# Second LoRA products and the mLSTM broadcast in float32r parts in a hybrid RWKV-7 / mLSTM trunk

## The chip, the core and the metric

The kernel runs on one core of one Trainium2 chip. TensorE multiplies matrices, VectorE (DVE in the profile), ScalarE (ACT) and GpSimd (POOL) work element by element, and DMA queues, most of them fed by SyncE (SP), move data between DRAM and the on-chip memory. The metric is the device time of one execution in microseconds; times below are those of one core.

## What is computed

One layer of a streaming encoder for 2,048 prompt frames behind 16 meta tokens and for 8 streams of 16 new frames: a norm and a combined projection, RWKV-7 time mixing (8 heads of 64) beside an mLSTM (4 heads of 128), an output projection, and a gated feed-forward part. The parts that the change touches, cut from the reference:

```python
def rwkv7_mix(p, shift_prev, S0, mu, w0, w2, a0, a2, g2, ...):
    pm = p + (prev - p) * mu                      # prev: p one token earlier
    r, k, v = pm[..., :i1], pm[..., i1:i2], pm[..., i2:i3]
    wl, al, gl = pm[..., i3:i4], pm[..., i4:i5], pm[..., i5:]   # 64, 64, 128 columns
    w = -softplus(-(w0 + tanh(wl) @ w2)) - 0.5
    decay = exp(-exp(w))
    a = sigmoid(a0 + al @ a2)
    g = sigmoid(gl) @ g2
    ...
    S = S * w_t + sa * (kk_t * a_t) + v_t * k_t   # one token after the other

def mlstm_block(state, blk):
    ...
    inter = b + m[..., None]
    mt = maximum(inter, max(Dm, axis=-1))         # running maximum
    wi = exp(Dm - mt[..., None])
    s = einsum('bhtd,bhjd->bhtj', q, k) * wi
    ...
```

The products with `w2`, `a2` and `g2` are "the second LoRA products". `mt` enters the mLSTM's weights as one row that stands for all rows of a block, which the kernel brings about by a product on TensorE ("the broadcast").

## The kernel before

The kernel has two phases. The first computes both mixers and ends at about 1,865 us of the profile, the second the feed-forward part; the change touches the first alone. Its tokens are cut into six segments: segment 0 with the 8 streams and the first frames (272 columns, 320 with padding), segments 1 to 5 with 384. Each segment has four slots, and slot u handles one pair of RWKV heads. Pair and segment together are called a unit here, numbered 0 to 23 (unit 11 is pair 3 of segment 2).

Large products are made in float32r, a form of float32 whose products appear as one record each. An operand is split in two parts, `hi` (a cast to float32r) and `lo` (the rest), and hi x hi, hi x lo and lo x hi are added up in one bank (L320). Weights are split once, by a cast on ScalarE (L374) and a subtraction on VectorE, and the parts are kept in DRAM. A product of plain float32 operands, such as the second LoRA products (L627, L631, L635) and the broadcast (L955), appears as two records in the profile.

A unit runs through these steps:

- **Front** (`rwkv`): projections of k, r and v (L320), and the three second LoRA products: `pw` (L627) and `pa` (L631) with 64 rows each, `pg` (L635) with 128. Their weights `lw2` lie on the chip for the whole run. Their moving operands `lo1` and `lo2` are made at the segment's first slot.
- **Scores**: three groups of two chunks of 64 tokens. A group's scores come from TensorE through the one bank of ring `a` into a buffer `sc` of ring `scs` (six buffers); its diagonal 16 x 16 blocks are masked into `dg` (L718) and added up into `cm` (L720), both on VectorE.
- **Forward substitution**: the diagonal blocks go through DRAM to another layout (`ad`, L750, and `bt`, L751, both issued by SyncE), GpSimd inverts them in 15 steps of a product and a subtraction (L759, L761), and the result goes back through DRAM (`td`, L764, and `ct`, L766) into `TA` (GpSimd, L775 by the helper L259).
- **Levels** (`levels`): two steps that extend the inverses from 16 to 64 rows. TensorE multiplies `cL` and `TA` (L305), the product is copied into `wv` (two buffers, L252), and TensorE multiplies it with `TA` again. A unit of segments 1 to 5 has six `wv` tiles.
- **Chain** (`chain`): for each chunk in turn the products with the state, L826, L839 and L845. This part and the levels are written in the program at the start of the slot after the unit's own, ahead of the next unit's front.

The mLSTM part of a slot runs over blocks of 128 tokens (64 for part of segment 0). L954 makes the scores, L955 the broadcast: a column of the identity with 4 rows, repeated over the columns, times the 4 rows of `ng`. There are 76 broadcasts.

The order of the instructions on each engine is not written out: a scheduler decides it before the run from priorities, which the table `KN` moves by stage. On the chip each engine takes its instructions in that fixed order and waits where data or a buffer isn't ready. Tiles of one tag share a ring of buffers; a tile that takes a buffer waits until the last reader of the tile that had it before.

The lines on which the change acts most:

```python
T.matmul(pw[:, :m], lw2[0:64, 0, us], lo1[0:64, :m], start=True, stop=True)
T.matmul(pa[:, :m], lw2[64:128, 0, us], lo1[64:128, :m], start=True, stop=True)
T.matmul(pg[:, :m], lw2[:, 1, us], lo2[:, :m], start=True, stop=True)
dg = sp.tile([128, 2, 4, 16], F32, name="dg", tag="dg", bufs=1)
wv = sp.tile([128, 2, 64], F32, name="wv", tag="wv")
```

## Time and profile before

| | |
|---|---|
| time, median of 3 runs (lowest to highest) | 3524.24 us (3522.81 to 3527.25) |
| span of the profiled execution | 3507.6 us |
| TensorE busy | 3411.7 us, 97% of the span |
| VectorE, ScalarE, GpSimd busy | 2146.4, 1152.2 and 941.0 us |
| moved by DMA | 459.40 MB, 131 GB/s in the mean |
| chain that ended last | TensorE 86%, VectorE 6%, DMA 3% |

The span runs from the first to the last instruction of one profiled execution; the median is 16.6 us longer. A timeline gives the start and the duration of an instruction (or of several alike, with their count); since products overlap in TensorE's pipeline, what one costs is the distance from its start to the next start, not its duration. Windows give the busy time of the engines in a stretch and the granted clock, as a share of full speed.

### The profile page before, as it was taken

The page shows a single profiled execution, that of the slowest core. Times are in us where ns is not written, and L with a number is a line of the kernel's source. Part 1 is how long each engine was busy: PE and PEld are TensorE (multiplying, and loading weights), DVE is VectorE, ACT ScalarE, POOL GpSimd, SP SyncE. Part 2 cuts the span into 40 slices and gives each one's busy share as a digit, 9 for nine tenths or more (in the row PEclk, how much of TensorE's full clock was granted, in tenths as well). Part 3 has the DMA queues.
Part 4 walks back from the last instruction along what each step waited for, and adds up shares of the span by engine and source line. Part 5 has one row for each costly group of instructions (what it writes and reads, how often), then busy time and mean ns, then how long its engine had stood idle before and what let it go on. Part 6 is the DMA issues. An engine that isn't in the chain of part 4 may idle for free.

```text
span 3507.6 us, 63114 instructions
## 1 busy us (share of the span) xinstructions
PE 3411.7 (97%) x24228; PEld 3123.6 (89%) x24228; DVE 2146.4 (61%) x5529; ACT 1152.2 (33%) x2826; POOL 941.0 (27%) x2294
## 2 busy tenths in 40 slices
PE   7999999999999999999989999999999999999998
PEld 6776888888888888888878999999999999999998
DVE  7777767666665776766665555574545447454544
ACT  5443444333433343343332222232222223222222
POOL 2532335434334444434421000021000012010002
PEclk9888999999999999999988999999999999999999
DMA  8753666455455545545523222232222233212221
GB/s 307 252 172 109 218 221 202 150 171 179 148 164 172 174 151 186 184 142 195 167 85 110 76 79 73 73 113 84 67 66 67 66 127 111 66 48 67 67 67 63
DMA packets 187565, 459.40 MB, mean 131 GB/s; under 512 B 68320, under 2 KB 111744, under 8 KB 156800
## 3 DMA queue, kind: packets, MB, share of 16 engines
q1 hardware_dynamic: 136648, 187.25, 18.0%
q0 software_dynamic: 28080, 204.48, 17.6%
q10 hardware_dynamic: 22536, 63.63, 4.8%
q8 instruction: 191, 3.13, 0.4%
q14 instruction: 110, 0.90, 0.1%
HBM read 381.68 MB, written 73.63 MB: 130 GB/s over the span
## 4 chain that ended last, share of the span: by engine, by line
PE 86%; DVE 6%; DMA 3%; ACT 2%; issue 1%; POOL 1%; ACTq 0%; SPq 0%; POOLq 0%; DVEq 0%
PE ps_gm L320 43%; PE ps_iv L320 11%; PE ps_a L320 10%; PE ps_m L320 5%; PE ps_iv L305 2%; PE ps_a L712 2%; PE ps_ch L826 1%; PE ps_ch L845 1%; PE ps_ch L839 1%; PE ps_iv L810 1%; PE ps_m L955 1%; DVE w L259 1%; DMA xt<-in_x_dram 1%; PE ps_a L305 1%; PE ps_m L972 1%
## 5 line engine op out<-in xcount | busy, mean ns | idle before, releaser
L320 PE MATMUL ps_gm<-hhi,w 128*128 128x384 f32 (+1 forms) x2976 | 813.1, 345 | 7.4 <-ACT w L374 2.2
L320 PE MATMUL ps_gm<-h2hi,w 128*128 128x384 f32 (+1 forms) x2816 | 701.1, 327 | 0.2 <-ACT ub L1221 0.2
L320 PEld LDWEIGHTS ps_gm<-hhi,w 128*128 128x128 f32 x2976 | 540.8, 193 | 30.2 <-issue 5.5
L320 PE MATMUL ps_gm<-hlo,w 128*128 128x384 f32 (+1 forms) x1488 | 502.2, 338 | 3.0 <-DVE hlo L360 3.0
L320 PEld LDWEIGHTS ps_gm<-h2hi,w 128*128 128x128 f32 x2816 | 500.0, 188 | 0.9 <-ACT ub L1221 0.5
L320 PE MATMUL ps_gm<-h2lo,w 128*128 128x384 f32 (+1 forms) x1408 | 459.9, 327 | 0.0
L374 ACT CAST w<-wraw 128x1024 fp32r<-128x1024 f32 (+2 forms) x291 | 259.4, 892 | 455.8 <-PE ps_iv L320 243.0
L320 PE MATMUL ps_iv<-gh,w 128*128 128x384 f32 (+1 forms) x1410 | 361.2, 330 | 0.0
L320 PE MATMUL ps_a<-h2hi,w 128*128 128x384 f32 (+1 forms) x1408 | 358.0, 327 | 0.0
L259 DVE TENSOR_TENSOR w<-wraw,w 128x1024 fp32r<-128x1024 f32 (+2 forms) x291 | 301.0, 1035 | 64.4 <-ACT w L374 60.4
L320 PEld LDWEIGHTS ps_gm<-hlo,w 128*128 128x128 f32 x1488 | 287.3, 193 | 9.5 <-DVE hlo L360 3.4
L320 PEld LDWEIGHTS ps_gm<-h2lo,w 128*128 128x128 f32 x1408 | 264.9, 188 | 0.0
L320 PEld LDWEIGHTS ps_iv<-gh,w 128*128 128x128 f32 x1410 | 252.5, 188 | 0.0
L320 PEld LDWEIGHTS ps_a<-h2hi,w 128*128 128x128 f32 x1408 | 251.0, 188 | 0.1
L320 PE MATMUL ps_iv<-gw,w 128*128 128x384 f32 (+1 forms) x705 | 232.6, 330 | 0.0
L320 PE MATMUL ps_a<-h2lo,w 128*128 128x384 f32 (+1 forms) x704 | 230.5, 327 | 0.0
L1238 ACT ACTIVATE fth<-ac 128x384 f32<-128x384 f32 (+1 forms) x132 | 67.2, 510 | 398.1 <-DVE ac L1236 388.7
L1231 POOL COPY h_f<-ub 128x2 f32<-128x2 f32 x88 | 16.4, 187 | 636.7 <-DVE ub L252 403.9
L320 PE MATMUL ps_m<-gh,w 128*128 128x384 f32 (+1 forms) x702 | 186.0, 330 | 0.0
L1259 DVE TENSOR_TENSOR x<-x,ps_iv 128x384 f32<-128x384 f32 (+1 forms) x160 | 85.3, 533 | 161.4 <-PE ps_iv L320 161.0
L1234 DVE TENSOR_SCALAR ac<-ub,d_fw,d_fb 128x384 f32<-128x384 f32 (+1 forms) x154 | 68.5, 457 | 182.8 <-ACT ub L248 157.1
L320 PE MATMUL ps_gm<-yhi,w 128*128 128x384 f32 (+1 forms) x640 | 168.3, 336 | 1.0 <-ACT yhi L359 0.7
(385 smaller groups left out, 6357.5 us busy)
## 6 DMA issues: line engine op xcount, KB each, us to landing
w<-wc POOLq DMA_DIRECT2D x155, 1024.0 KB, 5.4
wraw<-in_w_up_dram SPq DMA_DIRECT2D x132, 512.0 KB, 3.6
wc<-w ACTq DMA_DIRECT2D x31, 1024.0 KB, 6.5
wraw<-in_w_down_dram SPq DMA_DIRECT2D x72, 256.0 KB, 2.6
wraw<-in_w_in_dram SPq DMA_DIRECT2D x31, 512.0 KB, 5.9
wraw<-in_w_down_dram SPq DMA_DIRECT2D x48, 320.0 KB, 2.9
xraw<-in_xT_dram SPq DMA_DIRECT2D x36, 384.0 KB, 3.3
xt<-in_x_dram SPq DMA_DIRECT2D x15, 512.0 KB, 6.6
```

The costliest lines, as they stand in the source:

```text
L259: (V if e[turn[name] % len(e)] == "V" else G).tensor_tensor(out, a, b, op=op)
L305: T.matmul(out[h:h + 64], lhsT[h:h + 64], rhs[h:h + 64], start=start, stop=stop)
L320: T.matmul(ps, w, x, start=i == 0, stop=i == len(seq) - 1)
L374: S.copy(hi[:, :nk], raw[:, :nk])
L712: T.matmul(psS[hs, i, X], kb[hs, X, cl(c)], ar[hs, h, :, cl(c)], start=True, stop=True)
L810: T.matmul(pp[hs, i], TA[hs, 0, i], sb(SC[c][hs].unsqueeze(1), h)[:, 0], start=True, stop=True)
L826: T.matmul(pd[hs, :64], ar[:, h, x, cl(c)], vz[:, h], start=True, stop=x == 0)
L839: T.matmul(pz[hs, :64], kb2[:, h], vz[:, h], start=True, stop=True)
L845: T.matmul(py[hs, :64], sc[hs, 64:128], vz[hs, h], start=False, stop=True)
L1234: V.tensor_scalar(av, view(2), fwh[:, 44 + f:45 + f], fbh[:, f:f + 1], op0=ALU.mult, op1=ALU.add)
L1238: S.activation(th[:, :n], ac[:, :n], AF.Tanh)
L1259: V.tensor_tensor(X[s][:, d, :n], X[s][:, d, :n], p, op=ALU.add)
```

## The change

It does five things.

1. The second LoRA products are made of float32r parts. At the start `prepare_lora` loads `lora` in four pieces, splits each and stores the parts in DRAM (`LW`). In each unit the parts are loaded again into `lwr` (one buffer). `pw` and `pa` become two products each with all 128 rows: one half of the rows holds the `hi` part of the activations and the other half the `lo` part, against the `hi` weights (twice) and the `lo` weights (once, with zeros in the other half). `pg` becomes three.
2. `lo1` and `lo2` become pairs of float32r tiles. They are made from a tile `lx`, which takes buffers of the tags `bf` and `sq`, by casts on ScalarE and subtractions on VectorE.
3. The broadcast takes `ng` as `hi` and `lo` parts, in rows 0 to 3 and 32 to 35 of a 64-row tile that is zero elsewhere, against a float32r column `selr` that has a one in both places.
4. Ring `scs` has five buffers instead of six.
5. `dg` takes its buffer from the ring of `wv` instead of one of its own.

The rest of the diff takes docstrings away and calls `prepare_lora()` behind `build_h0()`. The diff, cut:

```diff
- 'b_scs': 6,
+ 'b_scs': 5,
...
-        lw2 = kp.tile([128, 2, 512], F32, name="lw2")
-        nc.sync.dma_start(lw2, A["lora"])
+        LW = [dr.tile([128, 2, 3, 128], F32R, name=f"lw{u}") for u in range(4)]
+
+        def prepare_lora():
+
+            for u in range(4):
+                lw2 = sp.tile([128, 2, 128], F32, name="lw2", tag="TA", bufs=KN.get("b_TA", 4))
+                nc.sync.dma_start(lw2, A["lora"][:, :, u * 128:u * 128 + 128])
+                t = sp.tile([128, 2, 3, 128], F32R, name="lwt", tag="scs", bufs=KN.get("b_scs", 6))
+                for j, (a, b) in enumerate((HALF, HALF[::-1])):
+                    S.copy(t[a, 0, j], lw2[a, 0])
+                    S.copy(t[b, 0, j], lw2[a, 0])
+                    V.tensor_tensor(t[a, 1, j], lw2[a, 0], f32(t[a, 0, j]), op=ALU.subtract)
+                    G.memset(f32(t[b, 1, j]), 0.0)
+                S.copy(t[:, 0, 2], lw2[:, 1])
+                V.tensor_tensor(t[:, 1, 2], lw2[:, 1], f32(t[:, 0, 2]), op=ALU.subtract)
+                nc.scalar.dma_start(f32(LW[u][:]), f32(t))
...
-            V.tensor_scalar(ng[:, :m], ga[:, :m], -1.0, None, op0=ALU.mult)
+            V.tensor_scalar(ng[0:4, :m], ga[:, :m], -1.0, None, op0=ALU.mult)
+            V.scalar_tensor_tensor(ng[32:36, :m], ga[:, :m], -1.0, f32(ng[0:4, :m]), op0=ALU.mult, op1=ALU.subtract)
...
+            lwr = ep.tile([128, 2, 3, 128], F32R, name="lwr", tag="lwr", bufs=1)
+            nc.sync.dma_start(f32(lwr), f32(LW[u][:]))
             pw = pt("gm")
-            T.matmul(pw[:, :m], lw2[0:64, 0, us], lo1[0:64, :m], start=True, stop=True)
+            for i in range(2):
+                T.matmul(pw[:, :m], lwr[:, i, 0], lo1[0][:, :m], start=i == 0, stop=i == 1)
...
-            T.matmul(pa[:, :m], lw2[64:128, 0, us], lo1[64:128, :m], start=True, stop=True)
+            for i in range(2):
+                T.matmul(pa[:, :m], lwr[:, i, 1], lo1[1][:, :m], start=i == 0, stop=i == 1)
...
-            T.matmul(pg[:, :m], lw2[:, 1, us], lo2[:, :m], start=True, stop=True)
+            for i, (a, b) in enumerate(((0, 0), (0, 1), (1, 0))):
+                T.matmul(pg[:, :m], lwr[:, a, 2], lo2[b][:, :m], start=i == 0, stop=i == 2)
...
-                    dg = sp.tile([128, 2, 4, 16], F32, name="dg", tag="dg", bufs=1)
+                    dg = sp.tile([128, 2, 4, 16], F32, name="dg", tag="wv")
...
-                T.matmul(psS[:L, 1, :L], ident[32 * (s % 2):32 * (s % 2) + 4, 32 * (s % 2) + hd:32 * (s % 2) + hd + 1].to_broadcast([4, L]), ng[:, cc], start=True, stop=True)
+                T.matmul(psS[:L, 1, :L], selr[:, hd:hd + 1].to_broadcast([64, L]), ng[:, cc], start=True, stop=True)
...
-                    lo1 = et("lo1", NW, 1)
-                    shifted(load_w(A["w_in"][CT_WA], CT_WA), h, s, CT_WA, lo1)
-                    S.activation(lo1[0:64, :m], lo1[0:64, :m], AF.Tanh)
...
+                    lx = et("bf", NW, 1)
+                    lo1 = [ep.tile([128, NW], F32R, name=f"lo1{i}", tag=f"lo1{i}", bufs=1) for i in range(2)]
...
+                    for j, (a, b) in enumerate((HALF, HALF[::-1])):
+                        S.copy(lo1[j][a, :m], lx[a, :m])
+                        V.tensor_tensor(lo1[j][b, :m], lx[a, :m], f32(lo1[j][a, :m]), op=ALU.subtract)
```

The scheduler orders all engines anew, far beyond the changed lines. Three places show it. Lines of the changed kernel are some 1 to 30 higher: L320 is L321 there, L305 L306, L627, L631 and L635 are L651, L656 and L661, L718 and L720 are L744 and L746, L826, L839 and L845 are L852, L865 and L871.

TensorE, unit 17, the three LoRA products (`lo`, with a number, is a part of `lo1` or `lo2`, and `lw` the weights). Before:

```order
L320 MATMUL ps_gm<-hhi,w 128x384
L627 MATMUL ps_gm<-lo_15351,lw_129 128x384
L743 MATMUL ps_a<-rm,cst 128x384
L826 MATMUL ps_ch<-scs,ar 64x64 x4
L305 MATMUL ps_iv<-TA,cL 64x64 x4
L631 MATMUL ps_gm<-lo_15351,lw_129 128x384
L635 MATMUL ps_gm<-lo_15386,lw_129 128x384
L305 MATMUL ps_a<-cst,sq 64x1 x11
```
and after:

```order
L321 MATMUL ps_gm<-hhi,w 128x384
L651 MATMUL ps_gm<-lo_15555,lwr 128x384 x2
L852 MATMUL ps_ch<-scs,ar 64x64
L756 MATMUL ps_a<-cst,kb 128x128 x2
L756 MATMUL ps_a<-cst,vm 128x128
L852 MATMUL ps_ch<-scs,ar 64x64 x3
L836 MATMUL ps_iv<-scs,TA 64x128 x4
L306 MATMUL ps_iv<-TA,cL 64x64 x4
L656 MATMUL ps_gm<-lo_15556,lwr 128x384 x2
L661 MATMUL ps_gm<-lo_15557,lwr 128x384
L661 MATMUL ps_gm<-lo_15558,lwr 128x384
L661 MATMUL ps_gm<-lo_15557,lwr 128x384
```
Three rows of one product each (two records in the profile) have become seven products; the scores' transposes (L756) and chain and level products stand between `pw` and `pa` now.

VectorE, where unit 18's levels meet the scores of unit 19 (`wv` belongs to unit 18, `dg` and `cm` to unit 19, `scs`, `z`, `yn` and BN_STATS to the chain). Before, with the third `dg` of unit 19:

```order
L252 COPY scs<-ps_ch 64x64 x2
L252 COPY wv<-ps_iv 128x128
L528 SCALAR_TENSOR_TENSOR lo_19097<-pb,par,lo_19097 128x384
L259 TENSOR_TENSOR cL<-scs,cst 128x2x64
L716 SCALAR_TENSOR_TENSOR scs<-ps_a,r_18435,cst 128x128 x2
L723 TENSOR_TENSOR ar<-ps_a,cst 64x2x2x64 x2
L718 TENSOR_TENSOR dg<-scs,cst 128x128
L843 SCALAR_TENSOR_TENSOR z_18103<-ps_ch,pls,zf 128x64
L252 COPY scs<-z_16332 64x64
L720 TENSOR_REDUCE cm<-dg 128x32
L847 BN_STATS bst<-ps_ch 128x6
L806 TENSOR_TENSOR TA<-TA,ps_iv 128x128
```
and after, with the first, second and third:

```order
L253 COPY scs<-ps_ch 64x64 x2
L253 COPY wv<-ps_iv 128x128
L744 TENSOR_TENSOR dg<-scs,cst 128x128
L260 TENSOR_TENSOR cL<-scs,cst 128x2x64
L746 TENSOR_REDUCE cm<-dg 128x32
L744 TENSOR_TENSOR dg<-scs,cst 128x128
L1067 TENSOR_TENSOR xraw<-xraw,ps_gm 128x384
L869 SCALAR_TENSOR_TENSOR z_20250<-ps_ch,pls,zf 128x64
L746 TENSOR_REDUCE cm<-dg 128x32
L253 COPY scs<-z_18503 64x64
L873 BN_STATS bst<-ps_ch 128x6
L744 TENSOR_TENSOR dg<-scs,cst 128x128
```
Before, the row `wv` is the fourth of six, and the fifth and sixth follow 7 and 25 rows behind the last row shown. After, it is the sixth, and all three `dg` of the next unit come behind it.

TensorE, unit 18's chain from the end of its fourth chunk on (after: from the third chunk's end). Before:

```order
L845 MATMUL ps_ch<-scs 64x64
L839 MATMUL ps_ch<-scs 64x64 x2
L845 MATMUL ps_ch<-scs 64x64
L305 MATMUL ps_iv<-wv,TA 64x64 x4
L320 MATMUL ps_gm<-hhi,w 128x384 x2
L320 MATMUL ps_gm<-hlo,w 128x384
L320 MATMUL ps_gm<-hhi,w 128x384 x2
L320 MATMUL ps_gm<-hlo,w 128x384
L320 MATMUL ps_gm<-hhi,w 128x384 x2
L320 MATMUL ps_gm<-hlo,w 128x384
L320 MATMUL ps_gm<-hhi,w 128x384 x2
L320 MATMUL ps_gm<-hlo,w 128x384
```
and after:

```order
L852 MATMUL ps_ch<-scs,ar 64x64 x4
L306 MATMUL ps_iv<-wv,TA 64x64 x4
L871 MATMUL ps_ch<-scs 64x64
L865 MATMUL ps_ch<-scs 64x64 x2
L871 MATMUL ps_ch<-scs 64x64
L836 MATMUL ps_iv<-scs,TA 64x128 x4
L971 MATMUL ps_iv<-cst,vm 128x128
L971 MATMUL ps_iv<-cst,km 128x128
L852 MATMUL ps_ch<-scs,ar 64x64 x4
L971 MATMUL ps_iv<-cst,vm 128x128
L971 MATMUL ps_iv<-cst,km 128x128
L998 MATMUL ps_m<-vt,mw 128x129
```
Before, projections fill the place behind a chunk; after, chunks follow each other with a level's last products and a few small mLSTM products between them.

## Rows read from the trace of the kernel before

**Rows 1.** The page, first part: each engine's busy time, share of the span, instructions.

```profile
PE 3411.7 (97%) x24228; PEld 3123.6 (89%) x24228; DVE 2146.4 (61%) x5529; ACT 1152.2 (33%) x2826; POOL 941.0 (27%) x2294
```

**Rows 2.** Timeline of TensorE: start us, us, engine, line, tiles, shape, records.

```profile
1725.20 0.33 PE L320 MATMUL ps_gm<-hlo,w 128*128 128x384 f32 x1
1725.38 0.34 PE L320 MATMUL ps_gm<-hhi,w 128*128 128x384 f32 x1
1725.64 0.91 PE L627 MATMUL ps_gm<-lo,lw 64*128 64x384 f32 x2
1726.48 0.91 PE L743 MATMUL ps_a<-rm,cst 128*128 128x384 f32 x2
```

**Rows 3.** Groups by line, mixers, TensorE: records, then busy us and mean ns.

```profile
L955 PE MATMUL ps_m<-ngs,cst 4*128 4x128 f32 x128 | 31.7, 328 | 0.0
```

**Rows 4.** Timeline of TensorE around one broadcast at full clock.

```profile
505.08 0.48 PE L955 MATMUL ps_m<-ngs,cst 4*128 4x128 f32 x2
505.49 0.33 PE L730 MATMUL ps_a<-cst,vm 128*128 128x128 f32 x1
505.58 0.50 PE L320 MATMUL ps_gm<-yhi,w 128*128 128x272 f32 x2
```

**Rows 5.** Windows: us, busy us of PE, PEld, DVE, ACT, POOL (instructions); clock, DMA share, GB/s.

```profile
200.00:300.00 100.00, 91.91 (x713) 66.21 (x712) 77.08 (x295) 39.11 (x135) 44.12 (x130) 0.82 0.47 134
1400.00:1600.00 200.00, 199.00 (x1684) 170.91 (x1683) 137.61 (x433) 78.04 (x229) 84.46 (x218) 1.00 0.52 166
1760.00:1780.00 20.00, 16.49 (x147) 14.26 (x144) 15.12 (x41) 11.33 (x31) 3.78 (x6) 0.83 0.40 109
1780.00:1800.00 20.00, 14.83 (x108) 12.43 (x107) 10.31 (x27) 5.38 (x12) 11.73 (x36) 0.84 0.26 70
1820.00:1840.00 20.00, 16.69 (x122) 12.80 (x122) 10.37 (x39) 5.58 (x18) 5.41 (x10) 0.69 0.13 43
1840.00:1865.00 25.00, 24.92 (x211) 19.51 (x210) 12.60 (x53) 6.90 (x26) 1.69 (x3) 0.57 0.03 10
```

**Rows 6.** Timelines of DVE, SyncE, GpSimd and TensorE: unit 11's substitution; `wv`, unit 10's last.

```profile
894.45 0.36 DVE L720 TENSOR_REDUCE cm<-dg 128x32 f32<-128x128 f32 x1
...
894.83 0.37 SPq L750 DMA_DIRECT2D ad<-cm  x1
...
896.84 0.32 SPq L751 DMA_DIRECT2D bt<-ad  x1
...
898.59 0.21 POOL L759 TENSOR_TENSOR ttmp<-bt,tb 48x15 f32<-48x15 f32 x1 [2.34 <-DMA bt<-ad]
...
913.99 0.21 POOL L761 TENSOR_TENSOR tb<-tb,ttmp 48x15 f32<-48x15 f32 x1
...
919.12 0.29 DVE L252 COPY wv<-ps_iv 128x128 f32<-128x128 f32 x1
...
919.82 1.47 POOL L259 TENSOR_TENSOR TA<-ct,cst 128x128 f32<-128x128 f32 x4 [0.59 <-DMA ct<-td]
...
948.87 0.45 PE L305 MATMUL ps_iv<-TA,cL 64*64 64x64 f32 x8
```

**Rows 7.** The same of unit 13: SyncE's and GpSimd's timelines.

```profile
1042.98 0.37 SPq L750 DMA_DIRECT2D ad<-cm  x1
...
1046.82 0.34 SPq L751 DMA_DIRECT2D bt<-ad  x1
...
1054.13 0.20 POOL L759 TENSOR_TENSOR ttmp<-bt,tb 48x15 f32<-48x15 f32 x1 [8.10 <-DMA bt<-ad]
...
1080.55 2.18 POOL L259 TENSOR_TENSOR TA<-ct,cst 128x128 f32<-128x128 f32 x6 [3.58 <-DMA ct<-td]
```

**Rows 8.** Timeline of TensorE at the end of the mixers: starts of chain chunks.

```profile
1842.45 0.70 PE L826 MATMUL ps_ch<-scs,ar 128*64 128x64 f32 x8
...
1846.68 0.69 PE L826 MATMUL ps_ch<-scs,ar 128*64 128x64 f32 x8
```

**Rows 9.** Timeline of ScalarE at the start: the first weight cast.

```profile
15.22 1.04 ACT L374 CAST w<-wraw 128x1024 fp32r<-128x1024 f32 x1 [7.39 <-DMA wraw<-in_w_in_dram]
```

23 lines of the change are left out of this document (17 added, 6 removed).

## Prediction

> **What bounds the kernel now.** The first part of the page says it shortly: TensorE is busy for 97% of the span [rows 1], so what counts is the work that stands in its queue and the gaps in which it waits. The timeline of TensorE gives the price of each kind of product, as the distance from one start to the next: a 384-column float32r product with 128 rows takes 0.17 us (1725.20 to 1725.38), and the last one ahead of a 64-row product 0.26 (1725.38 to 1725.64), so a change of the array's shape costs about 0.09 [rows 2]. The windows show where TensorE waits: hardly at all between 1400 and 1600 us; 8 us of 100 early on; and 3.5, 5.2 and 3.3 us of three stretches of 20 near the end of the mixers, where the granted clock is 0.83, 0.84 and 0.69 of full speed (the lower of its two levels, 1.2 of 2.4 GHz, for part of the time) [rows 5]. The third thing to read is no TensorE time at all: the forward substitution, followed from the reduction of `dg` to the first product that needs its result [rows 6, 7].
>
> **Part 1, products of the second LoRA step: about -34 us.** Each of the 24 units (a pair of heads in a segment) has three float32 products. The first takes 0.84 us as two records (L627, 1725.64 to 1726.48) [rows 2]; the other two (L631, L635) have the same columns and are taken at the same price: 2.52 us. After the change there are 2 + 2 + 3 = 7 float32r products of 128 rows and the same columns, 7 x 0.173 = 1.21. Saved: 1.31 us in each of 20 units of 384 columns, 26; the four units of segment 0 have 320 columns, some at a lower clock, and give 2 more: -28. The two 64-row products also disappear as shapes: three changes at 0.09 in 24 units are -6.
>
> **Part 2, the broadcast: -15 us, at most -24.** It stands 76 times (64 of 128 columns and 12 of 64), each as two records [rows 3]. One of 128 columns takes 0.41 us [rows 4]. As float32r it is one record. No row of before shows a float32r product of 128 columns; by columns it would be 128/384 of 0.173, 0.06, and the nearest row, a one-record product of 128 columns right behind the broadcast (L730), takes 0.09 (505.49 to 505.58) [rows 4]. Since 64 rows aren't 128, the shape change of 0.09 may stay beside it. So 0.22 to 0.35 is saved 64 times and half of it 12 times, 15 to 24; I take -15, with the shape change.
>
> **Part 3, what is added beside TensorE: nothing on the path, +3 at the start.** VectorE and ScalarE get 18 subtractions and 18 casts of LoRA activations, six small subtractions, and SyncE gets 24 loads of `lwr`. The order of after puts each load a whole unit ahead of its use, and its buffer's last reader (the third gate product of the unit before) well ahead of the hops that stand behind it in SyncE's queue; if that cover were gone, one load would hold a hop for some 4 us. The 24 loads (128 x 768 values of 4 bytes, 9.4 MB in all) lie beside products that don't wait for data. At the start the first weight load stands two places later on SyncE, and ScalarE has 15 casts ahead of its first weight cast; it waited 7.4 us there for that load [rows 9], which hides most of them. Between +1 (one issue) and +6 (casts and three DMA issues unhidden): +3.
>
> **Part 4, `dg` in the ring of `wv`: the term that decides.** The diff gives `dg` the tag `wv`, whose ring has two buffers, where it had one of its own. So a unit's `dg` can't be written before the unit ahead has let go of its level products `wv`. Before, it was: the reduction of unit 11 ended at 894.81, while unit 10's last `wv` was written at 919.12; its first level product on TensorE began at 948.87, 28 us after the result was there [rows 6]. The order of after shows the turn on VectorE: all six `wv` of unit 18, and then the three `dg` of unit 19. From there the substitution has a latency of its own: reduction, `ad`, `bt`, 15 steps on GpSimd, `td`, `ct`, first pair of `TA`. For unit 11 it is 894.81 to 920.6 (the first pair ends 0.8 after the start at 919.82), 25.8 us [rows 6]; for unit 13 the hops alone are longer, 3.8 us (`ad`, 1042.98 to 1046.82) and 7.3 (`bt`, 1046.82 to 1054.13), and the first pair ends at 1081.3, 38.3 us after the start [rows 7]. Over units 4 to 23 the ends are 23.5 and 46.3, the median 32. None of it was urgent before.
>
> TensorE takes its queue in order, so what hides this latency in after is the work between the last `wv` product of unit n-1 and the first `cL` product of unit n. I added it up along the order of after, each row at its price from the trace of before: over units 5 to 21 it is 18.8 to 37.3 us, 30.3 in the mean (18.8 at unit 19, 20.5 at 15, 23.4 at 11, 26 at 7 and 8); 12.0 at unit 22 and 13.8 at 23, where nothing is left to fill in. The need is the latency and 2.3 us for the last `dg` and its reduction. Which latency? TensorE, when it waits, also stops asking for weights, so the queues should be as empty as at unit 11: I take 26. Then units 5 to 21 lose the sum of what is missing, **+27**; units 22 and 23 16.3 + 14.5 = 31, from which the 12 us of waiting that stand there already [rows 5] go off: **+19**. With 23.5 these are 15 and 14, with 30 57 and 27, with 32 79 and 31.
>
> The Trainium skill ("DMA: Bandwidth & Descriptors", Anatomy of one DMA) gives a DMA a fixed cost of about 2.0 us, for the path through GpSimd. Unit 11's hop `ad` agrees (894.83 to 896.84), unit 13's do not (3.8 and 7.3), so the fixed cost is a floor here and not the price. By the rule all units would stand where unit 11 stands, and the sum would be the one below; by unit 13's rows it would be over 150 us higher.
>
> **Part 5, the chain: +4.** With the substitution late, the order has put projections ahead of the levels and left little between the chunks of the chain: after unit 18's fourth chunk, before 21 projections, now six small products. At the end of the mixers, where little else is left, a chunk takes 4.2 us (1842.45 to 1846.68) [rows 8], at a granted clock of 0.57 [rows 5], and the work between chunks is as little as 2 us at units 6, 10, 14, 18, 21 and 22. That costs 14 to 36 us by itself; but it falls in the same interval as the wait for `TA` and lengthens it, so that most of it is the same wait: +4, up to +25. `b_scs` 5 makes the third score group wait for the first chunks of the chain ahead; `dg` waits longer than that already: 0.
>
> **Part 6, the clock: +20.** The stretches with gaps are those with the lower clock: 8.1 us of waiting and 0.82 in 100 us, 3.5 and 0.83 in 20 [rows 5]. Read so, a microsecond of waiting costs up to two more; where gaps are short and far apart, nothing. For 50 new microseconds I take 0.4 each. Bounds 0 and 50.
>
> **Sum**: -28 - 6 - 15 + 3 + 27 + 19 + 4 + 20 = **+24**. The profiled execution has a span of 3507.6, so 3531.6; the median of the runs, 3524.24, is 16.6 above that span, which I leave as it is: **3548 us**.
>
> **Rivals.** *The substitution fits (faster).* GpSimd's 15 steps took 15.6 us at unit 11 with weight loads issued between them [rows 6]; with hops of 2 us and steps undisturbed, the latency is 22 or less. Then units 5 to 21 lose 10, the last two 11 net, the chain 4, the clock 8: -49 + 3 + 33 = -13, 3511; without any stall in the steady part and at full clock about -40, 3484. For it: the waiting instructions have TensorE's silence for themselves. Against: no unit of 4 to 23 came below 23.5. It decides from a latency of about 23.5 on, where the sum is zero. *The two cancel (no change).* Latency 23.5 to 24.5: 3520 to 3529. *The latency stays what it was (much slower).* At the median, 32: -49 + 3 + 79 + 31 + 4 + 40 = +108, 3632. For it: half of the units; against: it was measured where nobody waited and loads were dense. *`dg` doesn't wait in fact*, because the levels end earlier in the new order: that would be the first rival at its far end; the order of VectorE speaks against it.
>
> **How the numbers follow.** Slower, by the sum as it stands or nearly so (latency 25 to 30, 3531 to 3600), 0.40; much slower 0.11; no change 0.16; faster 0.33. A measurement of this kernel can tell about 0.2%, 7 us, from no change. The range reaches from the far end of the first rival to a latency of 30 with its clock: 3488 to 3605; some 0.08 lies below and 0.11 above.
>
> **What would show it.** In the trace of after: the LoRA products 0.17 us apart, 1.2 us for a unit; the broadcast below 0.2; the reduction of `dg` right behind the last `wv` of the unit before; TensorE's longest waits in front of the `cL` products (L306) with `TA` as releaser, some 1 to 2 us a unit in the mean and 7 or more at units 15, 19, 22 and 23; a granted clock below 1.00 between 1200 and 1600. If those waits are missing, part 4 is wrong and the time is near 3490; if the clock stays at 1.00 beside them, part 6 is.

## The result, and the profile after

The changed kernel takes 3656.75 us (median of 4 runs, 3652.3 to 3658.69), the kernel before 3523.52 us beside it. The ratio is **1.0387** (95% interval 1.0363 to 1.0411): 133 us slower. The forecast was 3548 with a range up to 3605; the direction was right, and the size far too small. Of the rivals, "the latency stays what it was" (3632) comes nearest.

The page of the changed kernel, first and third part, answers to [rows 1]:

```profile
PE 3481.3 (95%) x24176; PEld 3208.4 (88%) x24176; DVE 2150.8 (59%) x5568; ACT 1170.6 (32%) x2864; POOL 954.3 (26%) x2302
...
DMA packets 192543, 470.43 MB, mean 129 GB/s; under 512 B 68816, under 2 KB 113264, under 8 KB 161776
```

TensorE is busy 70 us longer than before, although it has less to do, and idle 80 us longer; DMA moves 129 GB/s in the mean, as before (131). The timeline of TensorE (start us, us, line, tiles, shape, records) shows the first two LoRA products of a unit, which answer to [rows 2]:

```profile
1698.46 0.34 PE L321 MATMUL ps_gm<-hlo,w 128*128 128x384 f32 x1
1698.63 0.34 PE L321 MATMUL ps_gm<-hhi,w 128*128 128x384 f32 x1
1698.81 0.51 PE L651 MATMUL ps_gm<-lo,lwr 128*128 128x384 f32 x2
1699.25 0.33 PE L852 MATMUL ps_ch<-scs,ar 128*64 128x64 f32 x2
```

From 1698.81 to 1699.25 it takes 0.44 us for both records and the change of shape behind them, where the one float32 product took 0.84. The gate product of unit 16, three records with a 64-column chain product behind them, takes 0.61:

```profile
1292.01 0.69 PE L661 MATMUL ps_gm<-lo,lwr 128*128 128x384 f32 x3
1292.62 0.46 PE L852 MATMUL ps_ch<-scs,ar 128*64 128x64 f32 x8
```

Over units 4 to 23 the medians of `pw`, `pa` and `pg`, each from its first start to the next start behind it, are 0.44, 0.45 and 0.63 us, in sum 1.5, for 3 x 0.84 before. A record costs 0.17 to 0.18 us inside a group and mostly 0.26 to 0.28 where a product of another shape stands beside it; 59 of the 140 records cost about that much. The broadcast, which answers to [rows 4]:

```profile
914.61 0.38 PE L980 MATMUL ps_m<-rm,km 128*128 128x128 f32 x2
914.92 0.32 PE L981 MATMUL ps_m<-ngs,selr 64*128 64x128 f32 x1
915.18 0.45 PE L852 MATMUL ps_ch<-scs,ar 128*64 128x64 f32 x8
```

0.26 us (914.92 to 915.18) for 0.41 before. So the products are cheaper by far than before, if not quite as cheap as forecast (1.2 us for the three LoRA products, below 0.2 for the broadcast). The windows (us, busy us of PE, PEld, DVE, ACT and POOL, then the granted clock, DMA share, GB/s) answer to [rows 5]; the last three are the mixers in three parts:

```profile
200.00:300.00 100.00, 89.42 (x690) 68.03 (x687) 72.00 (x269) 40.95 (x136) 32.73 (x90) 0.75 0.47 152
1400.00:1600.00 200.00, 192.07 (x1483) 167.05 (x1483) 119.21 (x355) 67.34 (x196) 85.12 (x207) 0.97 0.57 185
0.00:400.00 400.00, 345.72 (x2517) 284.09 (x2518) 289.24 (x983) 169.94 (x482) 130.47 (x373) 0.83 0.60 205
400.00:1886.00 1486.00, 1401.39 (x11060) 1212.07 (x11060) 914.48 (x2828) 535.35 (x1559) 580.64 (x1410) 0.93 0.52 169
1886.00:2010.60 124.60, 108.61 (x852) 89.23 (x851) 78.81 (x239) 43.10 (x125) 39.01 (x97) 0.72 0.21 59
```

Before, the same three parts of the mixers were:

```profile
0.00:400.00 400.00, 359.07 (x2677) 288.14 (x2678) 296.47 (x996) 172.87 (x491) 141.15 (x398) 0.90 0.62 206
400.00:1737.00 1337.00, 1315.78 (x10906) 1121.53 (x10904) 900.79 (x2776) 513.11 (x1510) 565.36 (x1401) 0.99 0.55 177
1737.00:1862.40 125.40, 112.20 (x898) 92.51 (x898) 80.97 (x240) 44.00 (x127) 31.02 (x74) 0.81 0.28 83
```

They had 40.9, 21.2 and 13.2 us of waiting at a clock of 0.90, 0.99 and 0.81. Now they have 54.3, 84.6 and 16.0 us at 0.83, 0.93 and 0.72. The feed-forward phase behind takes 1646.3 us in both profiles within 1.1 us (3656.9 - 2010.6 and 3507.6 - 1862.4), so everything happened in the mixers.

The balance of the mixers, which the table below repeats for every run, goes like this. Their length less the waiting, less what the clock took (one minus the granted clock, times the length of each part; with two digits of clock some 7 us are uncertain), leaves the work at full clock:

| | before | after | difference |
|---|---|---|---|
| length of the mixers, us | 1862.4 | 2010.6 | +148 |
| TensorE waits | 75 | 155 | +80 |
| taken by the clock | 77 | 207 | +130 |
| what remains | 1710 | 1649 | -61 |

The table counts time in which TensorE waits at a lower clock twice, as waiting and as clock. By the same windows (waiting of each part times one minus its clock) that is 7 us before and 20 after. Counted once, the clock took 70 and 187 us, 117 more, and the work at full clock is about 1717 and 1669 us, 48 less, where the forecast had 46 for products, broadcast and start.

The profiled execution of before was one of its shorter ones (its runs go from 3508 to 3536 us over all comparisons), that of after a longer one; hence 148 here and 133 in the medians.

The substitution of unit 12 with its neighbours, which answers to [rows 6] (DVE, SyncE, GpSimd; lines L746, L776, L777, L785, L787, L260 and L253 do what L720, L750, L751, L759, L761, L259 and L252 did):

```profile
1055.29 0.29 DVE L253 COPY wv<-ps_iv 128x128 f32<-128x128 f32 x1
...
1059.96 0.63 DVE L746 TENSOR_REDUCE cm<-dg 128x32 f32<-128x128 f32 x2
...
1060.62 0.37 SPq L776 DMA_DIRECT2D ad<-cm  x1
1062.60 0.32 SPq L777 DMA_DIRECT2D bt<-ad  x1
...
1066.59 0.21 POOL L785 TENSOR_TENSOR ttmp<-bt,tb 48x15 f32<-48x15 f32 x1 [3.44 <-DMA bt<-ad]
...
1086.60 0.21 POOL L787 TENSOR_TENSOR tb<-tb,ttmp 48x15 f32<-48x15 f32 x1
...
1093.71 2.19 POOL L260 TENSOR_TENSOR TA<-ct,cst 128x128 f32<-128x128 f32 x6 [2.13 <-DMA ct<-td]
...
1098.16 0.28 DVE L253 COPY wv<-ps_iv 128x128 f32<-128x128 f32 x1
...
1146.08 0.29 DVE L253 COPY wv<-ps_iv 128x128 f32<-128x128 f32 x1 [1.03 <-PE ps_iv L306]
```

The last `wv` of unit 11 is written at 1055.29, and the last of the three reductions of unit 12 (the rows show the second and third as one) ends at 1060.6, 5.3 us behind. 33.9 us later the first pair of `TA` is there (1094.5), and 3.7 us after that the first `wv` of unit 12 (1098.16). Its last one follows at 1146.08. Over units 6 to 21 the means of these four stretches are 5.2, 32.6, 3.2 and 41.3 us, in sum 82.3, which is the distance between units (82.4). Before, the first was -20.8 (the reduction came that much ahead of the last `wv`), the third 20.6, and the distance 74.5: the substitution stood beside the work of other units, and now it stands in a ring with the levels.

The list of TensorE's waits between 400 and 2011 us (line waited, releaser: us in total, times, longest):

```profile
PE ps_a L738 <- ACT scs L249: 17.2, 11, 2.5
PE ps_iv L306 <- POOL TA L260: 9.8, 5, 4.0
PE ps_a L756 <- DVE ar L749: 7.7, 9, 2.3
PE ps_gm L321 <- ACT pb L249: 5.8, 4, 3.2
```

The wait for `TA` is there, but it is 10 us. The other additional waiting is spread over scores, projections and the chain, in pieces of up to 3 us.

### The profile page after: what moved, and what is told of

It is laid out like the page before. It is cut to its first block, busy times and chain, and to the rows that moved or that the text cites. A ratio compares the mean times of both kernels' runs of the same rounds, so it can differ in the third digit from the quotient of the medians.

```text
span 3656.9 us, 63339 instructions
## 1 busy us (share of the span) xinstructions
PE 3481.3 (95%) x24176; PEld 3208.4 (88%) x24176; DVE 2150.8 (59%) x5568; ACT 1170.6 (32%) x2864; POOL 954.3 (26%) x2302
## 4 chain that ended last, share of the span: by engine, by line
PE 80%; DMA 6%; DVE 5%; POOL 4%; ACT 3%; issue 2%; SPq 0%; POOLq 0%; ACTq 0%; DVEq 0%
PE ps_gm L321 39%; PE ps_iv L321 10%; PE ps_a L321 10%; PE ps_m L321 5%; PE ps_iv L306 2%; PE ps_ch L852 1%; PE ps_a L738 1%; PE ps_ch L871 1%; POOL tb L787 1%; POOL ttmp L785 1%; PE ps_iv L836 1%; PE ps_ch L865 1%; ACT scs L251 1%; DMA td<-tb 1%; DMA xd<-xraw 1%
## 5 line engine op out<-in xcount | busy, mean ns | idle before, releaser
L321 PE MATMUL ps_gm<-hhi,w 128*128 128x384 f32 (+1 forms) x2976 | 816.0, 348 | 30.3 <-ACT w L375 10.5
L321 PE MATMUL ps_gm<-h2hi,w 128*128 128x384 f32 (+1 forms) x2816 | 703.8, 328 | 0.3 <-ACT ub L1255 0.2
L321 PEld LDWEIGHTS ps_gm<-hhi,w 128*128 128x128 f32 x2976 | 554.0, 197 | 53.7 <-ACT w L375 11.7
L321 PE MATMUL ps_gm<-hlo,w 128*128 128x384 f32 (+1 forms) x1488 | 510.1, 343 | 0.0
L321 PEld LDWEIGHTS ps_gm<-h2hi,w 128*128 128x128 f32 x2816 | 501.7, 189 | 1.1 <-ACT ub L1255 0.5
L321 PE MATMUL ps_gm<-h2lo,w 128*128 128x384 f32 (+1 forms) x1408 | 461.1, 328 | 0.0
L321 PE MATMUL ps_iv<-gh,w 128*128 128x384 f32 (+1 forms) x1410 | 361.2, 330 | 0.0
L321 PE MATMUL ps_a<-h2hi,w 128*128 128x384 f32 (+1 forms) x1408 | 357.4, 327 | 0.1
L260 DVE TENSOR_TENSOR w<-wraw,w 128x1024 fp32r<-128x1024 f32 (+2 forms) x291 | 302.3, 1039 | 52.1 <-ACT w L375 48.0
L321 PEld LDWEIGHTS ps_gm<-hlo,w 128*128 128x128 f32 x1488 | 294.1, 198 | 4.5 <-issue 1.3
L321 PEld LDWEIGHTS ps_gm<-h2lo,w 128*128 128x128 f32 x1408 | 265.8, 189 | 0.1
L321 PEld LDWEIGHTS ps_iv<-gh,w 128*128 128x128 f32 x1410 | 252.5, 188 | 0.0
L321 PEld LDWEIGHTS ps_a<-h2hi,w 128*128 128x128 f32 x1408 | 250.8, 188 | 0.2 <-DVE bo L771 0.2
L321 PE MATMUL ps_iv<-gw,w 128*128 128x384 f32 (+1 forms) x705 | 232.6, 330 | 0.0
L321 PE MATMUL ps_a<-h2lo,w 128*128 128x384 f32 (+1 forms) x704 | 230.3, 327 | 0.0
L321 PE MATMUL ps_m<-gh,w 128*128 128x384 f32 (+1 forms) x702 | 185.9, 330 | 0.0
L321 PE MATMUL ps_gm<-yhi,w 128*128 128x384 f32 (+1 forms) x640 | 176.8, 347 | 6.3 <-ACT yhi L360 5.8
L1293 DVE TENSOR_TENSOR x<-x,ps_iv 128x384 f32<-128x384 f32 (+1 forms) x160 | 85.2, 533 | 161.3 <-PE ps_iv L321 161.0
L371 POOL DMA_DIRECT2D w<-wc x155 | 92.0, 594 | 327.2 <-PE ps_gm L321 286.2
```

The costliest lines, as they stand in the source:

```text
L260: (V if e[turn[name] % len(e)] == "V" else G).tensor_tensor(out, a, b, op=op)
L321: T.matmul(ps, w, x, start=i == 0, stop=i == len(seq) - 1)
L371: nc.gpsimd.dma_start(w, WC[cache][:])
L1293: V.tensor_tensor(X[s][:, d, :n], X[s][:, d, :n], p, op=ALU.add)
```

## The experiments

Theory A was that `dg` in the ring of `wv` is the cause, theory B that the missing score buffer is, theory C that it is neither but the newly made order. Each ratio is against the kernel before on the same chip. The last three columns are the balance of the mixers as in the table above, with waiting at a lower clock in both of the first two of them.

| run | us | ratio (95%) | waits | clock | remains |
|---|---|---|---|---|---|
| changed kernel | 3656.8 | 1.0387 (1.0363-1.0411) | 155 | 207 | 1649 |
| e1 five score buffers | 3541.5 | 1.0066 (1.0042-1.0091) | 92 | 95 | 1714 |
| e2 `dg` in the ring of `wv` | 3642.5 | 1.0350 (1.0327-1.0372) | 139 | 154 | 1702 |
| e3 both | 3659.1 | 1.0402 (1.0378-1.0427) | 137 | 178 | 1701 |
| e4 changed, `dg` own | 3545.2 | 1.0068 (1.0038-1.0098) | 116 | 96 | 1681 |
| e5 most new products, old buffers | 3535.4 | 1.0044 (1.0032-1.0056) | 109 | 107 | 1673 |
| e6 broadcast alone | 3543.7 | 1.0066 (1.0050-1.0081) | 85 | 107 | 1694 |
| e7 hop in before | 3531.7 | 1.0028 (1.0015-1.0041) | 83 | 91 | 1706 |
| e8 hop in changed | 3678.8 | 1.0448 (1.0432-1.0464) | 172 | 194 | 1655 |
| e9 broadcast's control | 3519.5 | 1.0002 (0.9988-1.0017) | 81 | 81 | 1701 |
| e10 `pw`, `pa` alone | 3527.3 | 1.0024 (1.0010-1.0037) | 97 | 108 | 1676 |
| e11 e5, start eased | 3542.0 | 1.0058 (1.0043-1.0073) | 111 | 118 | 1663 |
| e12 ring of three | 3637.9 | 1.0321 (1.0292-1.0351) | 153 | 190 | 1646 |
| e13 before, other order | 3545.5 | 1.0075 (1.0050-1.0099) | 89 | 116 | 1704 |
| e14 e9, other order | 3549.2 | 1.0085 (1.0065-1.0106) | 85 | 108 | 1714 |
| e15 e6, other order | 3556.7 | 1.0102 (1.0079-1.0124) | 90 | 105 | 1700 |
| e16 e5, other order | 3515.9 | 0.9995 (0.9981-1.0008) | 92 | 92 | 1675 |
| e17 e16, start eased | 3517.5 | 0.9994 (0.9980-1.0009) | 103 | 123 | 1653 |
| e18 e10, other order | 3536.3 | 1.0034 (1.0018-1.0050) | 105 | 102 | 1677 |

### The two buffers (e1 to e4, e12)

```diff
# e1, in the kernel before
- 'b_scs': 6,
+ 'b_scs': 5,
# e2, in the kernel before; e3 has both
-                    dg = sp.tile([128, 2, 4, 16], F32, name="dg", tag="dg", bufs=1)
+                    dg = sp.tile([128, 2, 4, 16], F32, name="dg", tag="wv")
```

> The kernel before with one edit: five score buffers instead of six; products, weights and dg's own buffer as before. Theory A (the shared ring of dg and wv is what costs): the third score group now waits for the first two chunks of the unit ahead, but the reduction still comes two wv ahead of the last one, so little is lost: 3510 to 3550. Theory B (the missing score buffer closes the loop: third scores, reduction, substitution, levels, first two chunks, next third scores): most of the loss is here already, 3600 to 3670. Theory C (neither wait, only the newly shuffled order): no direction, within 30 us of 3524.

> The kernel before with the other edit alone: dg takes its buffer from the ring of wv; six score buffers. Theory A: the reduction follows the last wv of the unit ahead, the substitution's latency of 26 to 32 us is no longer covered, 3600 to 3670, with TensorE's waits in front of the cL products. Theory B: the third scores are early as before, and the loss is small, 3510 to 3560. Theory C: within 30 us of 3524.

> The kernel before with both buffer edits, and none of the new products. Theories A and B: the changed kernel's 3657 without its gain on products (25 to 50 us), so 3660 to 3710. Theory C: within 50 us of 3524; then the loss would lie in what the new products and loads bring.

e1 is 24 us slower, e2 125, e3 141: with no new product in it, e3 is as slow as the changed kernel. e2 takes the time that theory A gave it, e3 a microsecond less than A and B had at the least, and e1 lies within the range that theories A and C gave it, far below B's. e1's 24 us, and the 17 that e3 lies above e2, are no more than a newly made order moved by itself (27 us in e13, below), so a price of the sixth score buffer isn't shown by them. e2's balance against before is 64 us of waiting, 77 by the clock (67 counted once) and no change in the work:

```profile
0.00:400.00 400.00, 353.00 (x2524) 282.37 (x2525) 281.88 (x960) 161.65 (x455) 130.14 (x365) 0.84 0.57 195
400.00:1870.00 1470.00, 1404.05 (x11144) 1193.18 (x11142) 910.96 (x2819) 529.30 (x1554) 578.90 (x1411) 0.96 0.51 166
1870.00:1995.00 125.00, 98.94 (x811) 80.38 (x811) 75.87 (x233) 41.50 (x120) 39.85 (x96) 0.75 0.18 51
```

In e2 unit 12 looks as in the changed kernel (the third reduction behind the last `wv` of unit 11, 34 us to `TA`, and the next `wv` 3 us later):

```profile
1056.67 0.29 DVE L252 COPY wv<-ps_iv 128x128 f32<-128x128 f32 x1
...
1059.37 0.63 DVE L720 TENSOR_REDUCE cm<-dg 128x32 f32<-128x128 f32 x2
...
1093.11 2.15 POOL L259 TENSOR_TENSOR TA<-ct,cst 128x128 f32<-128x128 f32 x5 [4.07 <-DMA ct<-td]
...
1096.74 0.28 DVE L252 COPY wv<-ps_iv 128x128 f32<-128x128 f32 x1
```

In all of units 6 to 21 the three `dg` stand behind all six `wv` of the unit ahead on VectorE, in e2 as in the changed kernel; in before the third `dg` stood behind two to four of them. The waits are of the same kind, too: 16.0 us in front of the scores and 7.6 for `TA`, with six score buffers.

e4 takes `dg` out of the ring again in the changed kernel:

```diff
-                    dg = sp.tile([128, 2, 4, 16], F32, name="dg", tag="wv")
+                    dg = sp.tile([128, 2, 4, 16], F32, name="dg", tag="dg", bufs=1)
...
-        ngs = [kp.tile([64, NW], F32R, name=f"ngs{i}") for i in range(2)]
-        for t in ngs:
-            V.memset(f32(t), 0.0)
+        ngs = kp.tile([128, NW], F32R, name="ngs")
+        V.memset(f32(ngs), 0.0)
...
-            ng = ngs[s % 2]
+            ng = ngs[64 * (s % 2):64 * (s % 2) + 64]
```

> The changed kernel with dg in a buffer of its own again, five score buffers left; room for it comes from holding the broadcast's rows in one tile, rows 0 to 63 for even and 64 to 127 for odd segments. Theory A: the wait for the last wv is gone and the gain on products shows, 3480 to 3540. Theory B: the score buffer still closes the loop, 3600 to 3660. Both causes alike: between, 3550 to 3600.

112 us come back, to 3545, 5 us above theory A's range and below the other two. The same rows of unit 12 (reduction, last `wv` of unit 11, `TA`, first `wv` of unit 12):

```profile
1006.84 0.37 DVE L745 TENSOR_REDUCE cm<-dg 128x32 f32<-128x128 f32 x1
...
1019.93 0.29 DVE L253 COPY wv<-ps_iv 128x128 f32<-128x128 f32 x1
...
1039.94 1.11 POOL L260 TENSOR_TENSOR TA<-ct,cst 128x128 f32<-128x128 f32 x3
...
1045.40 0.28 DVE L253 COPY wv<-ps_iv 128x128 f32<-128x128 f32 x1
```

The reduction is 12.7 us ahead of the last `wv` (1007.2 and 1019.9), and `TA` lies ready 4.7 us before its use instead of 3.7; over 16 units these are 12.3 and 9.6 in the mean. It isn't as far ahead as before the change (20.8 and 20.6). That comes with five score buffers: e1 has 13.1 and 11.5, and every kernel here with six and a `dg` of its own has the reduction 19 to 23 us ahead. Yet `TA` is ready in time in e1 and e4, so the shorter lead doesn't explain why they are slower than before. 3545 is near e1, and no gain on products shows in it; e5 and the runs behind it look for that gain.

In e12 the shared ring has three buffers, as many bytes as in e4:

```diff
-                    dg = sp.tile([128, 2, 4, 16], F32, name="dg", tag="wv")
+                    dg = sp.tile([128, 2, 4, 16], F32, name="dg", tag="wv", bufs=3)
...
-                            wv = sp.tile([128, 2, 64], F32, name="wv", tag="wv")
+                            wv = sp.tile([128, 2, 64], F32, name="wv", tag="wv", bufs=3)
```

> The changed kernel with three buffers instead of two in the ring that dg and wv share (as many bytes as dg's own buffer of e4 takes; the broadcast's rows in one tile for room). If the loss comes from the place in the ring (the third dg takes the buffer of the last wv of the unit ahead, however deep the ring is up to three), nothing is won: 3635 to 3665. Rival (the ring was only too small for two users): near e4, 3535 to 3580.

3638, as for a wrong place in the ring and not for short room. If buffers are taken in turn, the third `dg` takes that of the last `wv` where there are three; where there are two, the second `dg` does, and the third stands behind it. That is argued from the rule of the ring; what the trace shows is that in units 6 to 21 all three `dg` still stand behind all six `wv`. By the rule the first `dg` could have come after the fourth, and why it doesn't isn't settled, nor was a ring of four tried. The last `wv` of unit 11 and the third reduction of unit 12, 5.4 us apart as in the changed kernel:

```profile
1059.04 0.29 DVE L253 COPY wv<-ps_iv 128x128 f32<-128x128 f32 x1
...
1064.14 0.34 DVE L745 TENSOR_REDUCE cm<-dg 128x32 f32<-128x128 f32 x1
```

### The latency by itself (e7, e8)

```diff
+                nc.sync.dma_start(ad2[:nch], ad[:nch])
-                nc.sync.dma_start(bt[:nb].rearrange("q i j -> q (i j)"), ad[:nch].rearrange("c (g i) j -> (c g) (i j)", i=16))
+                nc.sync.dma_start(bt[:nb].rearrange("q i j -> q (i j)"), ad2[:nch].rearrange("c (g i) j -> (c g) (i j)", i=16))
```

> The kernel before with one more hop in the substitution: ad is copied to a second place in DRAM before bt reads it, 24 times, 2 to 5 us each. Before, the result lay ready 12 to 33 us ahead of its use: if that slack is real, within 12 us of before. Rival (the substitution's latency counts in both kernels): 48 to 120 us slower.

> The changed kernel with the same additional hop. Theory A (its substitution is on the path, from the last wv of the unit ahead to the first cL product): 2 to 5 us in each of some 20 units, 40 to 100, and the clock's share on top, 3700 to 3800. Rival (the wait for TA is not what bounds it): within 20 us of 3657.

In before the hop costs 11 us, in the changed kernel 22. The first expectation is just met (within 12). In the second theory A's 40 to 100 isn't met, and the rival's "within 20" nearly is, which speaks against a time that follows the latency one for one. The hop lengthened the latency of before by 4.4 us in the mean (32.2 to 36.6), and `TA` was still ready 16.1 us ahead of its use. It lengthened that of the changed kernel by 2.8 us (32.6 to 35.4), 45 us over 16 units; the distance between units stayed at 82.0 (82.4 without it), because the other stretches shrank, the one from the first `wv` to the last from 41.3 to 39.6. So the ring of waits isn't stiff, and the picture of the prediction, where each missing microsecond of cover is a microsecond of waiting in front of `cL`, is too simple. Where e8's 22 us lie, and what the additional waiting is made of run by run, these experiments don't tell.

### Where the gain on products goes (e5, e6, e9 to e11, e13 to e18)

Theory D, in the expectations of these runs, is that a newly made order moves the time by 10 to 30 us whatever the edit; rival E is that the float32r products bring the loss with them.

e5 has the buffers of before with most of the new products; `pg` stays float32, its weights being loaded with the others:

```diff
 # against the changed kernel; dg and the broadcast's rows as in e4
- 'b_scs': 5,
+ 'b_scs': 6,
...
-            for i, (a, b) in enumerate(((0, 0), (0, 1), (1, 0))):
-                T.matmul(pg[:, :m], lwr[:, a, 2], lo2[b][:, :m], start=i == 0, stop=i == 2)
+            T.matmul(pg[:, :m], f32(lwr[:, 4, 0]), lo2[:, :m], start=True, stop=True)
```

> The new products with the buffers of before: pw, pa and the broadcast in float32r parts, six score buffers, dg's own buffer. To make room the gate product pg stays float32 (its weights are loaded with the others), and the broadcast's rows share one tile. On products this saves 24 x 2 x (0.84 - 0.35) = 23.5 us, some 5 for shapes, and 76 broadcasts at 0.41 - 0.25 give 11: 39, less 4 to 5 at the start: about -34. Theory A (the loss lay in the buffers, above all dg's): 3480 to 3500. Rival (the new order and the loads eat the gain wherever they stand): within 10 us of before or slower.

e6 has the broadcast alone, e9 the same with the product in float32, e10 `pw` and `pa` alone, e11 the start of e5 eased:

```diff
 # e6, in the kernel before
+            V.scalar_tensor_tensor(ng[32:36, :m], ga[:, :m], -1.0, f32(ng[0:4, :m]), op0=ALU.mult, op1=ALU.subtract)
...
-                T.matmul(psS[:L, 1, :L], ident[32 * (s % 2):32 * (s % 2) + 4, 32 * (s % 2) + hd:32 * (s % 2) + hd + 1].to_broadcast([4, L]), ng[:, cc], start=True, stop=True)
+                T.matmul(psS[:L, 1, :L], selr[64 * (s % 2):64 * (s % 2) + 64, hd:hd + 1].to_broadcast([64, L]), ng[:, cc], start=True, stop=True)
 # e9: f32(selr) and f32(ng) in the last line
 # e11, in e5
+        tc.cur_priority += 1000
         prepare_lora()
+        tc.cur_priority -= 1000
```

> The kernel before with the broadcast alone in float32r parts; buffers and LoRA as before. From the changed kernel's trace a broadcast of 128 columns takes 0.25 us for 0.41: 64 x 0.16 + 12 x 0.08 = -11 us. If products count one for one while nothing waits: 3505 to 3518. Rival (each new shuffle of the order costs some 10 to 20 us by itself): 3520 to 3545.

> The control to the broadcast alone: the same additional vector work, the same 64-row tile, and so a like newly made order, but the product itself in float32 as before (two records). Theory D (a newly made order costs some 10 to 30 us, part waiting and part clock, whatever the edit): as slow as the broadcast alone or up to 11 us slower, 3540 to 3560. Rival E (the float32r product is what costs, by its effect on the clock): near before, 3515 to 3528.

> pw and pa alone in float32r parts, with the buffers of before and the broadcast as before (float32, 4 rows). Products save 24 x 2 x 0.49 = 23.5 us and some 5 for shapes; the start costs 4 to 5. Theory A without an order effect: 3495 to 3505. Theory D: 3510 to 3535.

> The kernel with most of the new products and the old buffers, with the preparation of the LoRA weights put later in the scheduler's preference, so that the first weights are loaded and cast a few places earlier. If the start costs 4 to 5 us of waiting and as much again in clock there, 5 to 10 us faster than without it: 3525 to 3530. Theory D: anything within 15 us of it, without direction.

e5 is 15 us slower than before instead of 34 faster, e6 23 slower instead of 11 faster, e10 6 slower instead of 23 faster. The remainder of the table shows the saved work each time (1673 and 1676 in e5 and e10 against 1710), and waiting and clock that have grown by as much or more. With waiting at a lower clock counted once, by the clock's intervals in each trace, the work is 1711 to 1720 us in before, e1 to e3, e7 and e13, 1678 and 1682 in e5 and e16, 1686 and 1688 in e10 and e18, and 1671 in the changed kernel; e9 and e14, which save no product, have 1705 and 1723, so some 9 us either way are uncertain. So the products save about what was expected, and waiting and clock take it back. e9, as fast as before, made it look as if the float32r product itself were to blame. The windows at the end of segment 0 spoke against that. First e6, then e9 (columns as above):

```profile
250.00:300.00 50.00, 45.66 (x370) 34.15 (x367) 37.19 (x135) 19.13 (x72) 20.58 (x59) 0.86 0.37 109
300.00:350.00 50.00, 47.98 (x250) 35.07 (x251) 28.71 (x96) 12.38 (x39) 9.52 (x22) 0.56 0.17 48
350.00:400.00 50.00, 49.20 (x337) 44.41 (x335) 35.19 (x95) 20.71 (x52) 12.93 (x29) 1.00 0.58 207
```

```profile
250.00:300.00 50.00, 45.25 (x365) 34.14 (x362) 36.73 (x135) 18.65 (x70) 19.07 (x60) 0.86 0.38 109
300.00:350.00 50.00, 47.83 (x330) 38.90 (x329) 35.22 (x118) 14.57 (x45) 12.07 (x29) 0.83 0.35 108
350.00:400.00 50.00, 50.00 (x334) 44.72 (x333) 32.50 (x87) 23.24 (x61) 13.82 (x37) 1.00 0.58 192
```

Between 300 and 350 us TensorE is as busy in both, 48 of 50 us, but at a granted clock of 0.56 in e6 and 0.83 in e9: e6 spent most of those 50 us at the lower level of 1.2 GHz, which (some 13 us by the two clocks) is half of the 24 us that e6 lies above e9. The four broadcasts in it take some 1 us together, so it isn't by their own time that that stretch differs. So e13 to e16 took before, e9, e6 and e5 through one and the same small change of the scheduler's preference, which makes another order and no other work:

```diff
- 'g1': 0,
+ 'g1': 20,
```

> The kernel before in another order (one stage of the mLSTM gates 20 places later in the scheduler's preference), nothing else. Theory D (orders differ by 10 to 30 us by chance, and the one of before is a good one): 3525 to 3550. Rival E (orders of this kind cost nothing; float32r does): 3515 to 3527.

> The float32 control of the broadcast (e9, 3519) in the same other order of preference. Theory D: anywhere from 3515 to 3550. Rival E: 3515 to 3527.

> The broadcast alone in float32r parts (e6, 3543) in the other order of preference. Theory D: not tied to e6; with a good order 3505 to 3520, 11 us below its control. Rival E: 3535 to 3550 again, 15 or more above its control e14.

> Most new products with the old buffers (e5, 3535) in the other order of preference. Theory D: anywhere from 3490 to 3550. Rival E: 3530 to 3545 again.

The other order costs the kernel before 27 us and the control e9 30; e15 is 7 us above its control where e6 was 24 above its own; and e5 becomes 19 us faster, as fast as before. So a newly made order moved the time by 9 to 30 us, up or down, in the pairs of this table, and the order of the kernel before is a good one among those seen. Rival E is not met: it had e13 and e14 at 3515 to 3527, and e16 at 3530 to 3545. e15 fits neither theory, and the broadcast in float32r parts was slower than its control in both orders; two orders are too few to exclude that it brings some loss. Theory D's ranges were wide, so that the runs within them say less than e13 and e14, where no product changed. The balances of e13 and e16 (windows of the three parts of the mixers; columns as above):

```profile
0.00:400.00 400.00, 357.47 (x2565) 290.55 (x2566) 287.10 (x966) 168.99 (x473) 124.85 (x368) 0.84 0.58 198
400.00:1784.00 1384.00, 1345.57 (x10877) 1144.77 (x10877) 903.35 (x2770) 519.14 (x1522) 560.84 (x1401) 0.97 0.53 172
1784.00:1908.50 124.50, 116.25 (x1043) 94.74 (x1040) 88.75 (x276) 48.39 (x138) 43.81 (x104) 0.92 0.32 100
```

```profile
0.00:400.00 400.00, 349.48 (x2553) 286.07 (x2554) 296.11 (x985) 173.18 (x496) 134.32 (x376) 0.86 0.61 206
400.00:1734.00 1334.00, 1304.05 (x10935) 1131.88 (x10934) 913.30 (x2809) 524.29 (x1536) 577.30 (x1424) 0.99 0.57 183
1734.00:1858.80 124.80, 113.72 (x919) 94.02 (x917) 80.78 (x247) 45.48 (x128) 35.35 (x81) 0.82 0.28 89
```

e13 waits 89 us and loses 116 to the clock, e16 92 and 92; the profile of e13 is of its slowest execution (3555.9 us) and that of e16 of its fastest (3509.0), so they lie further apart than the medians do. In the same preference the new products come out 30 us faster (3545.5 to 3515.9), near the 34 that were expected; against before as it stands, nothing is gained. Each kernel has an order of its own even at the same preference, so the 30 are one draw and not a price. e17 eases the start of e16, e18 takes e10 through the other order:

> e16 (most new products, old buffers, the other order of preference: 3516) with the preparation of the LoRA weights put later, as in e11. If the start's 4 to 5 us of waiting come back and the order stays as good: 3505 to 3512, below before. Theory D: anywhere from 3500 to 3545.

> pw and pa alone in float32r parts with the old buffers (e10, 3527) in the other order of preference. Its products save some 28 us against e13 (3545), less 4 to 5 at the start: 3520 if the order were worth the same in both. Theory D: 3500 to 3550.

3517.5 and 3536.3: the start brought nothing that could be told from the order, as in e11. No version was found that is faster than the kernel before by more than the measurement's uncertainty.

## Why the prediction was wrong, by its own steps

- **Part 1, LoRA products (-34): the price was right, the shapes were not.** A record costs 0.17 to 0.18 us between its like. But the new order set many of them beside products of another shape, at 0.26 to 0.28, so that a unit's three products take 1.5 us and not 1.2; by these starts some 24 us are saved. The work in the balance is too coarse to tell 24 from 34.
- **Part 2, the broadcast (-15): too much by 4 to 5 us.** It costs 0.25 to 0.26 us instead of 0.41, so -10 to -11; 0.19 had been taken, with the shape change.
- **Part 3, beside TensorE (+3 at the start): right within 2 us.** The 300th projection product starts at 89.8 us instead of 85.2. The loads of `lwr` made no wait of their own that shows.
- **Part 4, `dg` in the ring of `wv`: the wait was right, its latency and its price were not.** e2 measures the edit alone at +125 us, 64 of them waiting; the forecast had +27 and +19. The sentence that failed is "TensorE, when it waits, also stops asking for weights, so the queues should be as empty as at unit 11: I take 26". The latency stayed where it was: 32.6 us in the mean over 16 units, 32.2 before, at 129 GB/s for 131. The median of 32 stood in the prediction itself and was set aside for an argument that no row carried. With 32 its formula gave +79 and +31, more than the 80 us of waiting that came in all, so the formula is too stiff, as e8 showed; that 46 came no further from the mark is in part two errors against each other. The Trainium skill's fixed cost of about 2.0 us for one DMA, given for the path through GpSimd ("DMA: Bandwidth & Descriptors", Anatomy of one DMA), agrees again with the hop `ad` (1060.62 to 1062.60), and not with the next, `bt`, whose data GpSimd used 4.0 us after the issue.
- **Where the waiting would show: wrong in part.** It was to stand in front of `cL` with `TA` as releaser. That is 10 us of it. The order made for the new dependency has other work ahead of the levels; that the rest is the same waiting in many small pieces is likely, as e2 has it too, but not shown piece by piece.
- **Part 5, `b_scs` 5 at nothing: open.** e1 is 24 us slower and e3 17 above e2, but an order made anew moves as much. Shown is only that the reduction comes some 8 us later with five buffers where `dg` has its own (e1, e4).
- **Part 6, the clock (+20, at most 50): the step that missed most.** Beside 80 us of new waiting the clock took 117 us more in the profiles (130 as the table counts). The runs say it without a profile: the mean granted clock was 0.942 in the changed kernel and 0.970 in before, which over 3657 and 3524 us is 212 and 106 us. The rows had it: 8.1 us of waiting in 100 stood beside a clock of 0.82 [rows 5], more than one for one, and I took 0.4 with the argument that short gaps far apart cost nothing. They did not come free: between 400 and 1886 us the gaps are short (4 us at most), and the clock is 0.93 for 0.99.
- **The 16.6 us between span and median: misread.** Around the changed kernel's span lie 1.8 us (3656.9 and 3658.69). So the profile of before was evidently taken of an execution some 15 us shorter than the median, and the sum was made against it.
- **Left out altogether: the order by itself.** An order made anew, with no other work, moved the time by 27 us (e13). That is more than half of what the products save, and no row of one profile could have shown it.

Taken together, the forecast had -46 for the work, +50 for waiting (27, 19 and 4) and +20 for the clock. The two profiles have -48, +80 and +117. Of the 124 us that were missed between them, about 97 lie in the clock and 30 in the waiting. (The range began at 3488 although its first rival went down to 3484; nothing hangs on that.)

## What to carry to other kernels

Two stages that share a ring of buffers are tied together in the order in which they take them: before a small tile moves into another stage's ring, ask which tile it now waits for, and whether a long latency begins behind it. One buffer more in the ring didn't help (e12); 512 bytes a partition of its own did (e4). Take a latency from the rows as they stand, not from what the queues ought to do. Count TensorE's clock beside new waiting at what rows of the same kernel show: here 1.2 to 1.6 us for one in the five kernels with `dg` in the ring, and 0.5 to 3 in the others. And measure a second order of the same work before a gain or loss of less than 1% is ascribed to an edit.
